# Prompt delta rule in chunks of 128 tokens instead of 64, in a hybrid decoder step

## The chip, the core and the metric

The kernel runs on one core of a Trainium2 chip. The core has a matrix engine (TensorE, PE in the profile; PEld is its loading of weights), a vector engine (VectorE, DVE), a scalar engine (ScalarE, ACT), GpSimd (POOL) and SyncE (SP), whose queue issues most DMAs. The engines run side by side and wait for each other by semaphores. The metric is the device time of one execution in microseconds; the median of several runs counts.

## The reference: what is computed

One layer of a decoder step, for a prompt of 256 tokens and for 8 decode sequences of one token each. One input projection feeds two token mixers: a sparse attention (compressed, selected and sliding-window branches) and a gated delta rule of 8 heads with a convolution ahead. Each mixer's output is gated and projected, the two are merged by gates, and an output projection is added to the input. The change touches the delta rule of the prompt:

```
def step(S, xc):                       # one chunk of C tokens, C = 64
    qc, kc, vc, gc, bc = xc
    dec = jnp.cumsum(gc, axis=-1)
    L = jnp.exp(jnp.where(tril, dec[..., :, None] - dec[..., None, :], -jnp.inf))
    ...
    A = jnp.where(stril, jnp.einsum('bhik,bhjk->bhij', kb, kc) * L, 0.0)
    Tm = lax.linalg.triangular_solve(eye + A, ...)      # the inverse
    u = Tm @ vb
    w = Tm @ (kb * jnp.exp(dec)[..., None])
    vn = u - w @ S
    att = jnp.where(tril, jnp.einsum('bhik,bhjk->bhij', qc, kc) * L, 0.0)
    o = (qc * jnp.exp(dec)[..., None]) @ S + att @ vn
    S = S * jnp.exp(dl)[..., None] + jnp.einsum('bhck,bhcv->bhkv', kc * jnp.exp(dl - dec)[..., None], vn)
    return S, o
```

The result of the recurrence does not depend on the length of a chunk. Heads have 128 key and 128 value channels; all of it is fp32.

## The kernel before

The body of the program is one long stream of weights. Each half of a weight unit (128 columns, 8 blocks of 128 rows, 512 KB) is loaded by SP into one of three buffers `raw`, split by ScalarE and VectorE into a high and a low fp32r part (`hi`, L326, and `lo`, L327), and used in 24 matmuls of 128x128x264, `acc` in the profile. `main order` at the end of the program lists the halves; load runs four halves ahead, the split two.

Everything else is written as Python generators (`g_gdn` for the prompt's delta rule, `g_gdn_dec` for that of the decode sequences, others for attention). Between two parts of a half, `tick` lets each of them emit the next piece, up to its next `yield n`, which asks for n ticks of rest. A scheduler then orders the instructions of TensorE, VectorE and ScalarE; SP and GpSimd keep the order of the program. When the stream comes to the first unit of the output gate of the delta rule (`ev_z` with w = 1), all that is left of `g_gdn` and `g_gdn_dec` is emitted at once, since that unit needs `oB`, their result.

`g_gdn`, in its order, for two tiles `t` of 128 tokens with two chunks of 64 in each: decays by matmuls with masks (`tric`, `bones`); for each head `At` (A transposed) and `aT` (att transposed) from one PSUM tile `kk`; the inverses of the 32x32 diagonal blocks of A, on VectorE by rows, one block a partition, through DRAM and back into `U` (the transposed inverse) and `TI`; a merge of 32x32 blocks to 64x64 ones by two groups of products (`inv` in the profile, copies `P`); for each head u and w (PSUM tile `uw`: four matmuls); then the scan over four chunks, each in two groups of four heads: `vn` = u - w S, `dS` (the growth of the state), `og` (the output), with the state in `Sg`. In the profile the state stands under the name `prod`, and vn and `aT` share the tile `aT`.

In the scan a chunk's 64 tokens are 64 partitions. So vn uses weights of 128 rows and 64 columns, dS of 64 rows and 128 columns, the first product of og 128 rows and 64 columns, and its second 64 by 64:

```
mm(pv[rows, 128 * hh:128 * hh + 128], wT[:, h, tok], Sg[:, h, :])
...
mm(pS[:, 128 * hh:128 * hh + 128], ktk[rows, t, h, :], vn[rows, h, :])
...
if c:
    mm(po[rows, ...], qTg[:, h, tok], Sg[:, h, :], start=True, stop=False)
mm(po[rows, ...], aT[rows, t, h, :], vn[rows, h, :], start=c == 0, stop=True)
```

The scan's and the merge's PSUM tiles come from one pool of two (`PG`). `sw` and `vnb` in the rows are matmuls and transpositions of `g_gdn_dec`, whose states `sst` (1 MB each, four of them) SP loads.

Of the kernel before, what the change touches and what calls it, by code (L numbers as in the profile page):

```python
# [49 lines left out]
def shape_constants():  # L50
    c = Cols()
    p = np.arange(128)
    same = (p[:, None] // 64) == (p[None] // 64)
    c.add("ident", np.eye(128))
    c.add("ones", np.ones((128, 128)))
    c.add("tric", (p[:, None] <= p[None]) & same)
    c.add("bones", same)
    c.add("mlow", np.where((p[:, None] > p[None]) & same, 0.0, BIG))
    c.add("mup", np.where((p[:, None] <= p[None]) & same, 0.0, -BIG))
    k = np.arange(256)  # L60
    q = p + 128
    c.add("base", np.where(q[:, None] >= k[None], -(q[:, None] - k[None]), -BIG))
    kend = np.arange(15) * 16 + 31
    b15 = np.zeros((128, 2, 15))
    for t in range(2):
        d = (p + 128 * t)[:, None] - kend[None]
        b15[:, t] = np.where(d >= 0, -d, -BIG)
    c.add("base15", b15)
    slope = 2.0 ** -(np.arange(8) + 1.0)
    c.add("slp", np.broadcast_to(np.tile(slope, 2) / SCALE, (128, 16)))  # L70
    kendd = np.arange(NCMP) * 16 + 31
    sl64 = np.broadcast_to(slope.reshape(2, 1, 4), (2, NB, 4)).reshape(64)
    c.add("cmpb", -(PAST - kendd)[:, None] * sl64[None])
    row = np.arange(64)
    srow = slope[(row // 32) * 4 + row % 4]
    c.add("c64", srow[:, None] * np.arange(64)[None])
    c.add("wrow", srow[:, None] * (np.arange(8) * 64 - 512)[None])
    c.add("e64", (row[None] // 4) == np.arange(16)[:, None])
    c.add("sel", ((row[None, None] // 32) == np.arange(2)[None, :, None])
          & (((row[None, None] // 4) % 8) == np.arange(8)[:, None, None]))  # L80
    c.add("rmask", ((p[:, None] % 64) // 4) == np.arange(16)[None])
    c.add("e", (np.arange(120)[None] // 8) == np.arange(16)[:, None])
    cs = np.arange(NCMP) * 16
    ss = np.arange(33) * 64
    ov = np.minimum(cs[:, None] + 32, ss[None] + 64) - np.maximum(cs[:, None], ss[None])
    c.add("m", (np.clip(ov, 0, None) / 32.0)[:, 1:31])
    c.add("gm", np.eye(24))
    dm = np.zeros((128, 8, NB))
    for h in range(8):
        dm[32 + h, h] = 1  # L90
        dm[64 + h, h] = 1
    c.add("dm", dm)
    c.add("s13", np.broadcast_to(np.arange(13), (16, 13)))
    c.add("blk", np.broadcast_to(np.arange(1, 31), (16, 30)))
    c.add("tg", (np.arange(120) % 8)[:, None] + (np.arange(16)[None] // 8) * (160 * 16))
    return c
# [42 lines left out]
def program(tc, A):  # L139
# [36 lines left out]

    # constants
    cst = cp.tile([128, CST.n], F32, name="cst")
# [39 lines left out]

    # long-lived small tiles
    xh = st.tile([128, KC, TT], F32R, name="xh", tag="xh")  # L220
# [50 lines left out]

    # ---- x: rms norm, split
    def g_xnorm():
# [34 lines left out]

    # ---- streams
    def three(ps, wh, wl, h, l, start, stop, n):  # L310
# [165 lines left out]

    # ---- projections
    def ev_kvc(j):
# [150 lines left out]

    # ---- decode: compressed attention, selection, gathers  # L630
    def g_dec_cmp():
# [41 lines left out]
        del L["kcT"], L["vc"]  # L673
        # ranks
        sa = slot("selA", [16, 2, 30, 30])
# [296 lines left out]

    # ---- prompt attention
    def g_attn():
# [6 lines left out]
        kT, vt = L["kTa"], L["vt"]  # L981
        # compressed branch, all heads
        z = tp.tile([128, 2, 8, 15], F32, name="pz", tag="pz")
# [91 lines left out]

    # ---- gated delta net
    def ev_qkv(j):
# [75 lines left out]
    def g_gdn():  # L1153
# [8 lines left out]
        bed = tp.tile([128, 2, 8], F32, name="bed", tag="bed")  # L1162
        edl = tp.tile([128, 8, 4], F32, name="edl", tag="edl")
        pt = PG("dec")
        for t in range(2):
            mm(pt[:, 8 * t:8 * t + 8], C("tric"), gt[:, t, :])
            mm(pt[:, 16 + 8 * t:24 + 8 * t], C("bones"), gt[:, t, :])
        V.tensor_copy(dec, pt[:, 0:16].rearrange("p (t h) -> p t h", t=2))
# [4 lines left out]
        At = slot("At", [128, 2, 8, 128])  # L1173
        av_ = slot("aT", [128, 2, 1024])
        aT = av_[:, 0].rearrange("p (t h i) -> p t h i", t=2, h=8)
        vn = av_[:, 1].rearrange("p (h d) -> p h d", h=8)
        yield 7
        lm = {}
        for h in range(9):
            if h < 8:  # L1180
# [13 lines left out]
                S.activation(l2, l2, AF.Exp)  # L1194
                V.tensor_copy(edl[:, h, :], er.rearrange("p (c i) -> p c i", c=4)[:, :, 63])
                lm[h] = l1, l2, er
            yield
            if h:
                h1 = h - 1
                l1, l2, er = lm.pop(h1)  # L1200
                pk = PG("kk")
                for t in range(2):
                    sl = slice(128 * t, 128 * t + 128)
                    mm(pk[:, 128 * t:128 * t + 128], kTg[:, h1, sl], kTg[:, h1, sl])
                    mm(pk[:, 256 + 128 * t:384 + 128 * t], kTg[:, h1, sl], qTg[:, h1, sl])
                for t in range(2):
                    V.scalar_tensor_tensor(At[:, t, h1, :], pk[:, 128 * t:128 * t + 128], be[:, t, h1:h1 + 1], l1[:, t],
                                           ALU.mult, ALU.mult)
                for c in range(2):
                    pr = slice(64 * c, 64 * c + 64)  # L1210
                    V.tensor_mul(aT[pr, :, h1, :], pk[pr, 256:512].rearrange("p (t i) -> p t i", t=2)[:, :, pr],
                                 l2[pr, :, pr])
                V.tensor_tensor(qTg[:, h1, 0:TP], qTg[:, h1, 0:TP], er, ALU.mult)
            yield 4
        del L["qkv", 1], kTg
        # inverse of the 32x32 diagonal blocks, one block a partition
        ad = dp.tile([4, 16, 32, 32], F32, name="ad")
# [32 lines left out]
        for t in range(2):  # L1250
            for hg in range(2):
# [16 lines left out]
                for c in range(2):  # L1268
                    V.tensor_scalar(U[64 * c:64 * c + 32, t, 4 * hg:4 * hg + 4, 64 * c + 32:64 * c + 64],
                                    p2v[64 * c:64 * c + 32, :, c, :], -1.0, None, ALU.mult)  # L1270
        uu = vbt
        wT = slot("wT", [128, 8, 256])
# [14 lines left out]
        del L["vbt"]  # L1287
        # scan
        Sg = prod[:, 0:1024].rearrange("p (h d) -> p h d", h=8)
        oG = slot("oG", [128, 2, 8, 128])  # L1290
        for c in range(4):
            t, off = c // 2, 64 * (c % 2)
            rows = slice(off, off + 64)
            tok = slice(64 * c, 64 * c + 64)
            for hg in range(2):
                hs = slice(4 * hg, 4 * hg + 4)
                if c == 0:
                    V.tensor_copy(vn[rows, hs], uu[rows, t, hs])
                else:
                    pv = PG("vn")  # L1300
                    for hh in range(4):
                        h = 4 * hg + hh
                        mm(pv[rows, 128 * hh:128 * hh + 128], wT[:, h, tok], Sg[:, h, :])
                    V.tensor_sub(vn[rows, hs], uu[rows, t, hs], pv[rows, :].rearrange("p (h d) -> p h d", h=4))
            yield 6
            for hg in range(2):
                hs = slice(4 * hg, 4 * hg + 4)
                pS = PG("dS")
                for hh in range(4):
                    h = 4 * hg + hh  # L1310
                    mm(pS[:, 128 * hh:128 * hh + 128], ktk[rows, t, h, :], vn[rows, h, :])
                yield 6
                po = PG("og")
                for hh in range(4):
                    h = 4 * hg + hh
                    if c:
                        mm(po[rows, 128 * hh:128 * hh + 128], qTg[:, h, tok], Sg[:, h, :], start=True, stop=False)
                    mm(po[rows, 128 * hh:128 * hh + 128], aT[rows, t, h, :], vn[rows, h, :],
                       start=c == 0, stop=True)
                yield  # L1320
                for hh in range(4):
                    h = 4 * hg + hh
                    if c == 0:
                        V.tensor_copy(Sg[:, h, :], pS[:, 128 * hh:128 * hh + 128])
                    else:
                        V.scalar_tensor_tensor(Sg[:, h, :], Sg[:, h, :], edl[:, h, c:c + 1],
                                               pS[:, 128 * hh:128 * hh + 128], ALU.mult, ALU.add)
                for hh in range(4):
                    h = 4 * hg + hh
                    S.activation(oG[rows, t, h], po[rows, 128 * hh:128 * hh + 128], AF.Copy, scale=qss[rows, t, h:h + 1])  # L1330
                yield 4
# [122 lines left out]

    # ---- output side
    hl = {}
# [58 lines left out]

    # ---- main order
    halves = []
# [202 lines left out]
```

## Time and profile before

| | |
|---|---|
| median of 3 runs | 1166.74 us (1165.35 to 1169.48) |
| the profiled execution, its span | 1167.3 us |
| TensorE, matmul | 1135.1 us busy, 97% |
| TensorE, weight load | 1097.8 us, 94% |
| VectorE / ScalarE / GpSimd | 68% / 52% / 13% |
| chain that ended last | TensorE 82%, VectorE 5%, DMA 3% |
| HBM | 203 MB read, 18 MB written, 189 GB/s |

The shares are means over the whole span. The chain that ended last follows the work back from the last instruction; what stands in it, and not what is busy, sets the time. A busy TensorE is not TensorE at its peak: the ends of matmuls are modelled and neighbours overlap, so the start of one call to that of the next tells more than a duration. The line L199 is the helper `mm` and L196 the helper `tr` (transposition on TensorE), through which nearly all matmuls go; the groups have to be read by their tiles. A matmul in fp32 leaves two records, so "x8" is four of them.

### The profile page before, as it was taken

To read this page: it belongs to the slowest core of one execution; us is meant where nothing else is said; L and a number is where in the kernel's file an instruction comes from. 1 tells how busy PE (TensorE), PEld (TensorE's weight loads), DVE (VectorE), ACT (ScalarE), POOL (GpSimd) and SP (SyncE) were. 2 spreads that over 40 slices of the span, in tenths; PEclk is the share of its full clock that TensorE was granted. 3 is DMA by queue.
4 is the path that set the end of the run, shared out by engine and by line. 5 is a ranking of instruction groups with operands and counts; after the bars stand their busy time and mean duration, and the time that the engine had idled before them with its cause. 6 is when DMAs were issued, how large, how long until landed. Compare 5 with 4: busy or idle time off the path is not lost.

```text
span 1167.3 us, 24685 instructions
## 1 busy us (share of the span) xinstructions
PE 1135.1 (97%) x9136; PEld 1097.8 (94%) x9136; DVE 789.7 (68%) x1651; ACT 607.6 (52%) x1173; POOL 147.5 (13%) x218
## 2 busy tenths in 40 slices
PE   3999999999999999999899999998999999999998
PEld 3989999999999997998899999998998799999998
DVE  3487665443677876986888876899575665567543
ACT  4455655444635776875666554443345354344332
POOL 4420344100001221204112100100100000000000
PEclk9999999999999999999999999999999999999999
DMA  8874576334436865468887644554743345555663
GB/s 296 256 223 148 191 217 203 106 133 164 159 133 198 227 181 147 135 192 210 320 316 269 245 162 162 188 204 134 231 172 118 127 145 179 183 181 210 206 237 128
DMA packets 76844, 222.83 MB, mean 191 GB/s; under 512 B 10465, under 2 KB 27370, under 8 KB 75186
## 3 DMA queue, kind: packets, MB, share of 16 engines
q1 hardware_dynamic: 59922, 168.55, 42.7%
q0 software_dynamic: 14784, 45.68, 13.6%
q10 hardware_dynamic: 2016, 7.01, 1.5%
q8 instruction: 72, 1.18, 0.4%
q14 instruction: 50, 0.41, 0.1%
HBM read 203.21 MB, written 17.99 MB: 189 GB/s over the span
## 4 chain that ended last, share of the span: by engine, by line
PE 82%; DVE 5%; DMA 3%; issue 1%; POOL 1%; ACT 1%; SPq 0%; DVEq 0%; ACTq 0%; POOLq 0%
PE acc L199 66%; PE og L199 2%; DMA gv<-cslv,idx 2%; DVE lo L327 1%; DVE lanes L1234 1%; PE po L199 1%; PE gsc L199 1%; PE gtr L196 1%; PE sw L199 1%; DVE prod L1233 1%; PE ps L199 1%; PE pvo L199 1%; DMA raw<-win 1%; PE dS L199 1%; PE cf L199 1%
## 5 line engine op out<-in xcount | busy, mean ns | idle before, releaser
L326 ACT ACTIVATE hi<-raw 128x1024 fp32r<-128x1024 f32 (+1 forms) x250 | 264.1, 1056 | 324.2 <-PE acc L199 260.5
L199 PE MATMUL acc<-xh,hi 128*128 128x264 f32 (+1 forms) x1488 | 428.5, 288 | 1.4 <-DVE gate L1489 1.0
L199 PE MATMUL acc<-xl,hi 128*128 128x264 f32 (+1 forms) x1488 | 426.6, 287 | 0.0
L199 PE MATMUL acc<-xh,lo 128*128 128x264 f32 (+1 forms) x1488 | 425.9, 286 | 0.0
L327 DVE TENSOR_TENSOR lo<-raw,hi 128x1024 fp32r<-128x1024 f32 (+1 forms) x250 | 304.5, 1218 | 172.1 <-ACT hi L326 168.5
L199 PEld LDWEIGHTS acc<-xh,hi 128*128 128x128 f32 (+1 forms) x1488 | 280.3, 188 | 3.8 <-ACT hi L326 1.2
L199 PEld LDWEIGHTS acc<-xl,hi 128*128 128x128 f32 (+1 forms) x1488 | 280.4, 188 | 1.9 <-issue 0.7
L199 PEld LDWEIGHTS acc<-xh,lo 128*128 128x128 f32 (+1 forms) x1488 | 279.5, 188 | 2.0 <-issue 1.0
L199 PE MATMUL acc<-hi,w1h 128*128 128x254 f32 (+1 forms) x512 | 147.6, 289 | 16.5 <-ACT hi L403 16.5
L199 PE MATMUL acc<-lo,w1h 128*128 128x254 f32 (+1 forms) x512 | 146.4, 286 | 3.8 <-DVE lo L404 3.6
L199 PE MATMUL acc<-hi,w1l 128*128 128x254 f32 (+1 forms) x512 | 144.9, 283 | 0.0
L404 DVE TENSOR_TENSOR lo<-rawc,hi 128x512 fp32r<-128x512 f32 (+2 forms) x136 | 84.0, 656 | 51.1 <-ACT hi L403 45.3
L199 PEld LDWEIGHTS acc<-hi,w1h 128*128 128x128 f32 x512 | 97.8, 191 | 16.8 <-ACT hi L403 16.7
L403 ACT ACTIVATE hi<-rawc 128x512 fp32r<-128x512 f32 (+2 forms) x136 | 74.6, 599 | 58.6 <-PE acc L199 54.4
L199 PEld LDWEIGHTS acc<-lo,w1h 128*128 128x128 f32 x512 | 98.3, 192 | 5.1 <-DVE lo L404 4.9
L199 PEld LDWEIGHTS acc<-hi,w1l 128*128 128x128 f32 x512 | 98.3, 192 | 0.1
L380 POOL DMA_DIRECT2D rawc<-ccmp x125 | 67.4, 539 | 100.4 <-issue 70.0
L199 PE MATMUL acc<-oh,hi 128*128 128x264 f32 x256 | 72.9, 285 | 0.4 <-ACT gate L1482 0.4
L199 PE MATMUL acc<-ol,hi 128*128 128x264 f32 x256 | 72.7, 284 | 0.0
L199 PE MATMUL acc<-mh,hi 128*128 128x264 f32 x256 | 72.6, 284 | 0.0
L199 PE MATMUL acc<-oh,lo 128*128 128x264 f32 x256 | 72.6, 283 | 0.0
L199 PE MATMUL acc<-ml,hi 128*128 128x264 f32 x256 | 72.5, 283 | 0.0
(447 smaller groups left out, 1685.2 us busy)
## 6 DMA issues: line engine op xcount, KB each, us to landing
raw<-win SPq DMA_DIRECT2D x184, 512.0 KB, 3.8
raw<-wpab SPq DMA_DIRECT2D x32, 512.0 KB, 3.2
raw<-wo SPq DMA_DIRECT2D x32, 512.0 KB, 4.3
rawc<-ccmp SPq DMA_DIRECT2D x126, 128.0 KB, 3.1
rawc<-ccmp POOLq DMA_DIRECT2D x125, 128.0 KB, 3.1
raw<-w SPq DMA_DIRECT2D x8, 512.0 KB, 8.0
wk<-winK SPq DMA_DIRECT2D x8, 512.0 KB, 7.4
o_wk<-wk POOLq DMA_DIRECT2D x8, 512.0 KB, 7.8
```

Source lines behind the costliest of these rows:

```text
L196: T.transpose(out, in_, ident[0:n, 0:n])
L199: T.matmul(out, lhsT, rhs, start=start, stop=stop, **k)
L326: S.activation(self.hi, self.raw, AF.Copy)
L327: V.tensor_sub(self.lo, self.raw, self.hi)
L380: e.dma_start(rawc[kv, b][j // 8][:, j % 8].rearrange("p s c g -> p (s c g)"), src[kv, bass.ds(r, 1)].rearrange("o d f -> (o d) f"))
L403: S.activation(h, src, AF.Copy)
L404: V.tensor_sub(l, src, h)
L1233: V.tensor_tensor(pp, Lt[:, 0:i, 0:i], La[:, i, 0:i, None].to_broadcast([64, i, i]), ALU.mult)
L1234: V.tensor_reduce(Lt[:, i, 0:i], pp.rearrange("p j c -> p c j"), AX.X, ALU.add, negate=True)
```

## The change

The delta rule of the prompt works on chunks of 128 tokens, so a chunk is a whole tile.

- The masks are those of 128 tokens; `bones` is replaced by the existing `ones`. `aT` holds 128x128 for each tile and head, and its product with the decays is one VectorE instruction instead of two.
- The inverse gets one more merge, of 64x64 blocks to 128x128: for each tile and each half of the heads four matmuls and four transpositions of 64x64, two copies on ScalarE (`P1`, `T1`), four matmuls of 64x64, and a negating copy on VectorE into `U`.
- The scan has two chunks instead of four, with all 128 partitions. The first chunk needs no vn; the one step that depends on a state is that of the second. vn is written in place into u (`uu`, in the profile `vbt`), the copy of the first chunk's u is gone, and the state of the first chunk is copied for four heads at once.
- The yields are others: 112 ticks of rest in the scan become 40, and 16 come with the merge.

```diff
-    c.add("tric", (p[:, None] <= p[None]) & same)
-    c.add("bones", same)
-    c.add("mlow", np.where((p[:, None] > p[None]) & same, 0.0, BIG))
-    c.add("mup", np.where((p[:, None] <= p[None]) & same, 0.0, -BIG))
+    c.add("tric", p[:, None] <= p[None])
+    c.add("mlow", np.where(p[:, None] > p[None], 0.0, BIG))
+    c.add("mup", np.where(p[:, None] <= p[None], 0.0, -BIG))
...
-                for c in range(2):
-                    pr = slice(64 * c, 64 * c + 64)
-                    V.tensor_mul(aT[pr, :, h1, :], pk[pr, 256:512].rearrange("p (t i) -> p t i", t=2)[:, :, pr],
-                                 l2[pr, :, pr])
+                V.tensor_mul(aT[:, :, h1, :], pk[:, 256:512].rearrange("p (t i) -> p t i", t=2), l2)
...
+        for t in range(2):
+            for hg in range(2):
+                p1 = PG("inv")
+                for hh in range(4):
+                    h = 4 * hg + hh
+                    mm(p1[0:64, 256 + 64 * hh:320 + 64 * hh], At[64:128, t, h, 0:64], U[64:128, t, h, 64:128])
+                for hh in range(4):
+                    tr(p1[0:64, 64 * hh:64 * hh + 64], U[0:64, t, 4 * hg + hh, 0:64])
+                yield 2
+                P1 = tp.tile([128, 256], F32, name="P1", tag="a", bufs=NA)
+                T1 = tp.tile([128, 256], F32, name="T1", tag="a", bufs=NA)
+                S.activation(P1[0:64], p1[0:64, 256:512], AF.Copy)
+                S.activation(T1[0:64], p1[0:64, 0:256], AF.Copy)
+                yield 2
+                p2 = PG("inv")
+                for hh in range(4):
+                    o = slice(64 * hh, 64 * hh + 64)
+                    mm(p2[0:64, o], T1[0:64, o], P1[0:64, o])
+                V.tensor_scalar(U[0:64, t, 4 * hg:4 * hg + 4, 64:128], p2[0:64, 0:256].rearrange("p (h j) -> p h j", h=4),
+                                -1.0, None, ALU.mult)
...
-        for c in range(4):
-            t, off = c // 2, 64 * (c % 2)
-            rows = slice(off, off + 64)
-            tok = slice(64 * c, 64 * c + 64)
...
+        for t in range(2):
+            tok = slice(128 * t, 128 * t + 128)
+            if t:
...
-                        mm(pv[rows, 128 * hh:128 * hh + 128], wT[:, h, tok], Sg[:, h, :])
-                    V.tensor_sub(vn[rows, hs], uu[rows, t, hs], pv[rows, :].rearrange("p (h d) -> p h d", h=4))
-            yield 6
+                        mm(pv[:, 128 * hh:128 * hh + 128], wT[:, h, tok], Sg[:, h, :])
+                    V.tensor_sub(uu[:, t, hs], uu[:, t, hs], pv.rearrange("p (h d) -> p h d", h=4))
+                yield 4
+            vn = uu[:, t]
...
-                    mm(pS[:, 128 * hh:128 * hh + 128], ktk[rows, t, h, :], vn[rows, h, :])
-                yield 6
+                    mm(pS[:, 128 * hh:128 * hh + 128], ktk[:, t, h, :], vn[:, h, :])
+                yield 4
...
-                    if c:
-                        mm(po[rows, 128 * hh:128 * hh + 128], qTg[:, h, tok], Sg[:, h, :], start=True, stop=False)
-                    mm(po[rows, 128 * hh:128 * hh + 128], aT[rows, t, h, :], vn[rows, h, :],
-                       start=c == 0, stop=True)
+                    if t:
+                        mm(po[:, 128 * hh:128 * hh + 128], qTg[:, h, tok], Sg[:, h, :], start=True, stop=False)
+                    mm(po[:, 128 * hh:128 * hh + 128], aT[:, t, h, :], vn[:, h, :], start=t == 0, stop=True)
```

How the instructions stand on the engines after scheduling. On TensorE, where the old merge ends and the products with `U` begin, the program before has:

```order
L199 MATMUL inv<-P_12769,prod 32x32 x8
L199 MATMUL uw<-vbt,U 128x128
L199 MATMUL uw<-U,kbe 128x128
L199 MATMUL uw<-vbt,U 128x128
L199 MATMUL uw<-U,kbe 128x128
L199 MATMUL acc<-ol,hi 128x264
```

After the change the new level begins there. This is its first round, and the start of the stream behind it:

```order
L197 MATMUL inv<-P_12761,prod 32x32 x8
L197 MATMUL inv<-U,At 64x64 x4
L194 MATMUL inv<-cst,U 64x64 x4
L197 MATMUL acc<-ol,hi 128x264
L197 MATMUL acc<-oh,lo 128x264
```

and the place where its last products (P and T are the copies P1 and T1) lead on to uw:

```order
L197 MATMUL inv<-P_13023,T_13024 64x64 x4
L197 MATMUL uw<-vbt,U 128x128
L197 MATMUL uw<-U,kbe 128x128
L197 MATMUL uw<-vbt,U 128x128
L197 MATMUL uw<-U,kbe 128x128
L197 MATMUL acc<-xh,hi 128x264
```

The first uw has moved behind four rounds of the new level. Between a round's first group and its last stand 26 acc calls, and the last products of the first three rounds stand together with the first of the next. The last uw comes 44 acc calls later than before. On TensorE in the scan, the first chunk that has a state stands before as:

```order
L199 MATMUL vn<-prod,wT 64x128 x4
L199 MATMUL sw<-wq,sst 128x64 x5
L199 MATMUL vn<-prod,wT 64x128 x4
L199 MATMUL sw<-wq,sst 128x64 x6
L199 MATMUL dS<-aT,ktk 128x128 x4
L199 MATMUL sw<-wq,sst 128x64 x3
L199 MATMUL og<-prod,qkvr 64x128
L199 MATMUL og<-aT 64x128
```

and after the change, where it is the only chunk that has one:

```order
L197 MATMUL sw<-wq,sst 128x64 x11
L197 MATMUL vn<-prod,wT 128x128 x4
L197 MATMUL dS<-vbt,ktk 128x128 x4
L197 MATMUL sw<-wq,sst 128x64 x5
L194 MATMUL vnb<-cst,dvn 128x128 x4
L197 MATMUL og<-prod,qkvr 128x128
L197 MATMUL og<-vbt,aT 128x128
```

The sizes are those of the output: 64 partitions have become 128. Such a place stands three times in the program before and once after. On SP's queue, where the second to fourth decode states are loaded ahead of the next weight halves, with the semaphores that each load waits for, before:

```order
L321 DMA raw<-win 128x1024 [waits DMAHW7_49,DVE_49]
L1414 DMA sst<-stS 128x2048 [waits DMASW3_49,DMASW4_49,DMASW2_49,DMASW6_49,DMASW1_49,DMASW7_49,DMASW0_49,PE_49]
L1414 DMA sst<-stS 128x2048 [waits DMASW5_49,PE_49]
L1414 DMA sst<-stS 128x2048 [waits DMASW4_49,DMASW3_49,DMASW5_49,DMASW2_49,DMASW7_49,DMASW0_49,PE_49]
L321 DMA raw<-win 128x1024 [waits DMAHW0_49,DVE_49]
```

and after:

```order
L319 DMA raw<-win 128x1024 [waits DMAHW7_49,DVE_49]
L1423 DMA sst<-stS 128x2048 [waits DMASW5_49,DMASW4_49,DMASW6_49,DMASW3_49,PE_49]
L1423 DMA sst<-stS 128x2048 [waits DMASW3_49,DMASW4_49,DMASW2_49,DMASW6_49,DMASW1_49,DMASW7_49,DMASW0_49,PE_49]
L1423 DMA sst<-stS 128x2048 [waits DMASW3_49,DMASW4_49,DMASW2_49,DMASW5_49,DMASW0_49,DMASW7_49,DVE_49,PE_49]
L319 DMA raw<-win 128x1024 [waits DMAHW0_49,Activation_49]
```

The order on SP is unchanged. The third of these loads goes, before and after, into the buffer of `U`, and so waits for the last uw on TensorE; the buffers of the first two have changed (after: that of an old weight operand, and that of `At`). The first half behind them is the same half, and its first acc call the same call, in both programs.

## Rows read from the trace of the kernel before

**Rows 1.** The page's engine line: busy us, share of the span, instructions.

```profile
PE 1135.1 (97%) x9136; PEld 1097.8 (94%) x9136; DVE 789.7 (68%) x1651; ACT 607.6 (52%) x1173; POOL 147.5 (13%) x218
```

**Rows 2.** Windows: merge and uw, scan, rest; us busy by engine, granted clock, DMA.

```profile
832.00:872.00 40.00, 39.57 (x382) 38.85 (x383) 26.05 (x69) 19.12 (x39) 0.00 (x0) 1.00 0.45 162
872.00:941.00 69.00, 69.00 (x499) 56.30 (x499) 40.74 (x123) 30.80 (x98) 0.17 (x1) 1.00 0.34 129
941.00:1167.00 226.00, 223.13 (x1848) 222.92 (x1846) 128.45 (x173) 95.75 (x128) 0.40 (x1) 1.00 0.54 187
```

**Rows 3.** Timeline of TensorE at one uw: start us, us, what, count of records.

```profile
858.35 0.28 PE L199 MATMUL acc<-xh,lo 128*128 128x264 f32 x1
858.47 0.38 PE L199 MATMUL uw<-vbt,U 128*128 128x128 f32 x2
...
859.49 0.28 PE L199 MATMUL acc<-xl,hi 128*128 128x264 f32 x1
```

**Rows 4.** Timeline of TensorE at one dS group (64*128: rows and columns of weights).

```profile
872.06 0.28 PE L199 MATMUL acc<-xh,lo 128*128 128x264 f32 x1
872.27 1.16 PE L199 MATMUL dS<-aT,ktk 64*128 64x128 f32 x8
...
873.58 0.28 PE L199 MATMUL acc<-xl,hi 128*128 128x264 f32 x1
```

**Rows 5.** Timeline of TensorE at one vn group.

```profile
922.05 0.28 PE L199 MATMUL acc<-xh,lo 128*128 128x264 f32 x1
922.26 1.09 PE L199 MATMUL vn<-prod,wT 128*64 128x128 f32 x8
...
923.50 0.28 PE L199 MATMUL acc<-xl,hi 128*128 128x264 f32 x1
```

**Rows 6.** Timeline of TensorE at one og group with a state.

```profile
929.54 0.28 PE L199 MATMUL acc<-xl,hi 128*128 128x264 f32 x1
929.75 0.43 PE L199 MATMUL og<-prod,qkvr 128*64 128x128 f32 x2
930.12 0.43 PE L199 MATMUL og<-aT 64*64 64x128 f32 x2
...
932.87 0.28 PE L199 MATMUL acc<-xh,hi 128*128 128x264 f32 x1
```

**Rows 7.** Timeline of TensorE at eight transpositions of attention, 64 rows.

```profile
507.96 0.68 PE L196 MATMUL ptr<-cst,sb 64*120 64x64 f32 x8
...
508.80 0.28 PE L199 MATMUL acc<-xl,hi 128*128 128x264 f32 x1
```

**Rows 8.** Timeline of TensorE at four such transpositions.

```profile
628.49 0.46 PE L196 MATMUL ptr<-cst,wb 64*128 64x64 f32 x4
...
629.11 0.28 PE L199 MATMUL acc<-xl,hi 128*128 128x264 f32 x1
```

**Rows 9.** Timeline of TensorE in the old merge: eight 32x32 matmuls.

```profile
836.32 0.44 PE L199 MATMUL inv<-P,prod 32*32 32x32 f32 x16
836.69 1.10 PE L199 MATMUL inv<-U,At 128*128 128x64 f32 x8
```

**Rows 10.** Timeline of ScalarE in the old merge: a split, then the copy P.

```profile
833.66 1.06 ACT L326 ACTIVATE hi<-raw 128x1024 fp32r<-128x1024 f32 x1 [0.31 <-DMA raw<-win]
834.63 0.36 ACT L1259 ACTIVATE P<-inv 128x256 f32<-128x256 f32 x1
```

**Rows 11.** Waits of SP's queue, 640 to 1000 us: us, times, longest.

```profile
SPq L1414 <- PE sw L199: 12.6, 1, 12.6
```

**Rows 12.** Loads of decode states (tile sst), whole trace.

```profile
DMA to landing us min/median/max: 7.4/8.0/8.5
```

**Rows 13.** DMA issues, 840 to 960 us: weight halves, KB, median us to landing.

```profile
raw<-win SPq DMA_DIRECT2D x19, 512.0 KB, 3.3
```

**Rows 14.** The page's groups of the split: busy us, mean ns of one.

```profile
L326 ACT ACTIVATE hi<-raw 128x1024 fp32r<-128x1024 f32 (+1 forms) x250 | 264.1, 1056 | 324.2 <-PE acc L199 260.5
L327 DVE TENSOR_TENSOR lo<-raw,hi 128x1024 fp32r<-128x1024 f32 (+1 forms) x250 | 304.5, 1218 | 172.1 <-ACT hi L326 168.5
```

More of the change, by code (lines that the diff above doesn't have):

```diff
@@ L52, in shape_constants @@
     p = np.arange(128)
-    same = (p[:, None] // 64) == (p[None] // 64)
     c.add("ident", np.eye(128))
     c.add("ones", np.ones((128, 128)))
-    c.add("tric", (p[:, None] <= p[None]) & same)
-    c.add("bones", same)
-    c.add("mlow", np.where((p[:, None] > p[None]) & same, 0.0, BIG))
-    c.add("mup", np.where((p[:, None] <= p[None]) & same, 0.0, -BIG))
+    c.add("tric", p[:, None] <= p[None])
+    c.add("mlow", np.where(p[:, None] > p[None], 0.0, BIG))
+    c.add("mup", np.where(p[:, None] <= p[None], 0.0, -BIG))
     k = np.arange(256)
@@ L1162, in g_gdn @@
         bed = tp.tile([128, 2, 8], F32, name="bed", tag="bed")
-        edl = tp.tile([128, 8, 4], F32, name="edl", tag="edl")
+        edl = tp.tile([128, 8, 2], F32, name="edl", tag="edl")
         pt = PG("dec")
@@ L1166, in g_gdn @@
             mm(pt[:, 8 * t:8 * t + 8], C("tric"), gt[:, t, :])
-            mm(pt[:, 16 + 8 * t:24 + 8 * t], C("bones"), gt[:, t, :])
+            mm(pt[:, 16 + 8 * t:24 + 8 * t], ones, gt[:, t, :])
         V.tensor_copy(dec, pt[:, 0:16].rearrange("p (t h) -> p t h", t=2))
@@ L1173, in g_gdn @@
         At = slot("At", [128, 2, 8, 128])
-        av_ = slot("aT", [128, 2, 1024])
-        aT = av_[:, 0].rearrange("p (t h i) -> p t h i", t=2, h=8)
-        vn = av_[:, 1].rearrange("p (h d) -> p h d", h=8)
+        aT = slot("aT", [128, 2, 8, 128])
         yield 7
@@ L1194, in g_gdn @@
                 S.activation(l2, l2, AF.Exp)
-                V.tensor_copy(edl[:, h, :], er.rearrange("p (c i) -> p c i", c=4)[:, :, 63])
+                V.tensor_copy(edl[:, h, :], er.rearrange("p (c i) -> p c i", c=2)[:, :, 127])
                 lm[h] = l1, l2, er
@@ L1290, in g_gdn @@
         oG = slot("oG", [128, 2, 8, 128])
-        for c in range(4):
-            t, off = c // 2, 64 * (c % 2)
-            rows = slice(off, off + 64)
-            tok = slice(64 * c, 64 * c + 64)
[L1295 to L1299, printed above, removed]
+        for t in range(2):
+            tok = slice(128 * t, 128 * t + 128)
+            if t:
+                for hg in range(2):
+                    hs = slice(4 * hg, 4 * hg + 4)
                     pv = PG("vn")
@@ L1315, in g_gdn @@
                     h = 4 * hg + hh
-                    if c:
-                        mm(po[rows, 128 * hh:128 * hh + 128], qTg[:, h, tok], Sg[:, h, :], start=True, stop=False)
-                    mm(po[rows, 128 * hh:128 * hh + 128], aT[rows, t, h, :], vn[rows, h, :],
-                       start=c == 0, stop=True)
+                    if t:
+                        mm(po[:, 128 * hh:128 * hh + 128], qTg[:, h, tok], Sg[:, h, :], start=True, stop=False)
+                    mm(po[:, 128 * hh:128 * hh + 128], aT[:, t, h, :], vn[:, h, :], start=t == 0, stop=True)
                 yield
[L1321 to L1326, printed above, removed]
+                if t == 0:
+                    V.tensor_copy(Sg[:, hs, :], pS.rearrange("p (h d) -> p h d", h=4))
+                else:
+                    for hh in range(4):
+                        h = 4 * hg + hh
+                        V.scalar_tensor_tensor(Sg[:, h, :], Sg[:, h, :], edl[:, h, t:t + 1],
                                                pS[:, 128 * hh:128 * hh + 128], ALU.mult, ALU.add)
@@ L1329, in g_gdn @@
                     h = 4 * hg + hh
-                    S.activation(oG[rows, t, h], po[rows, 128 * hh:128 * hh + 128], AF.Copy, scale=qss[rows, t, h:h + 1])
+                    S.activation(oG[:, t, h], po[:, 128 * hh:128 * hh + 128], AF.Copy, scale=qss[:, t, h:h + 1])
                 yield 4
```

## The prediction, made before the changed kernel had run

> **What bounds the kernel now.** I read the engine line of the page first: TensorE is busy 1135 of 1167 us, the other engines far less [rows 1]. Then the stretch that the change touches, by windows: the merge of the inverse and the products behind it (832 to 872 us), the scan (872 to 941) and the rest. TensorE is busy 39.57 of 40, 69.00 of 69 and 223.13 of 226 us, at full granted clock, while in the scan VectorE works 40.74 and ScalarE 30.80 us of 69, and the DMA engines a third of the time [rows 2]. So TensorE's own time is the price here: a microsecond of matmul less is a microsecond less, as long as nothing else comes to be waited for. A busy TensorE says nothing on how dense its calls are, so I took the rest from the timeline, from start to start.
>
> The weight stream, in fp32r, starts a call each 0.12 us (858.35 to 858.47) [rows 3]. The fp32 calls of the delta rule stand between those. What a group costs is the start of the second acc call behind it, minus the start of the last acc ahead, minus two steps of 0.12: what the change from the one kind of call to the other costs on either side is then in it. Four full calls (128 rows, 128 columns of weights, 128 moving columns) cost 859.49 - 858.35 - 0.24 = **0.90** us [rows 3]. Four half-height calls cost more: dS, with 64 rows, 873.58 - 872.06 - 0.24 = **1.28** [rows 4]; vn, with 64 columns, 923.50 - 922.05 - 0.24 = **1.21** [rows 5]. Worst are the eight calls of og behind the first chunk, where a call of 128 rows and one of 64 alternate: 932.87 - 929.54 - 0.24 = **3.09**, at 0.37 from each call to the next (929.75 to 930.12) [rows 6].
>
> **The change, part by part.**
>
> *The scan.* Four chunks of two head groups before: vn 6 groups (three chunks have a state) x 1.21 = 7.3; dS 8 x 1.28 = 10.2; og of the first chunk 2 groups, which I price as vn (64 columns, as many calls), 2.4; og of the other three 6 x 3.09 = 18.5. Together 38.4. Some dS and og stand side by side and pay the way in and out once; I take 1 off: 37.4. Afterwards there are two chunks: vn 2 groups of four, dS 4, og 2, and 2 of eight, which is 12 groups of four, all with full weights and 128 moving columns, the form of rows 3: 12 x 0.90 = 10.8. **The scan gives 26.6 us.** The alternation in og stays, but both its calls now have the form of uw.
>
> At this place a rule speaks against the change. The Trainium skill (TensorE: Matmul & The Clock Gate, LDWEIGHTS) says that a weight load takes time by its columns, whatever its rows. By it the 64-column loads of vn and og would be cheaper than the full ones, where the trace has 1.21 against 0.90; I go by the trace, and carry the rule as a rival.
>
> *The new level.* For each tile of 128 tokens and half of the heads: four matmuls (64 rows, 64 columns, 64 moving) and four transpositions into one PSUM bank, two copies by ScalarE, four matmuls, one negating copy by VectorE. A matmul leaves two records on TensorE (four vn are x8), a transposition one. So a round is 8 + 4 + 8 = 20 records, four rounds 80. No row of before has this form. The nearest are transpositions of 64 rows and 64 moving columns: eight take 508.80 - 507.96 - 0.12 = 0.72 [rows 7], four 629.11 - 628.49 - 0.12 = 0.50 [rows 8]; so 0.055 a record, and 0.28 for a run, to which I add the 0.09 of a late entry (872.06 to 872.27 is 0.21, not 0.12 [rows 4]): 0.37. By the new order the rounds make five runs, since each last product stands with the first products of the next round. 80 x 0.055 + 5 x 0.37 = **6.3 us**. From below: 32x32 calls, 16 records in 836.69 - 836.32 = 0.37 us [rows 9], give 80 x 0.023 = 1.8. From above: the price of vn, 0.151 a record, gives 12.1. I take 6.3, as rows and moving columns are equal there.
>
> *Waits that the level may add.* The order has 26 acc calls, 3.1 us, between a round's first products and its last. In that time ScalarE must make two copies. In the merge of before one such copy took 0.36 and began straight behind a 1.06 us weight split [rows 10]; two copies behind one split are 1.8 us. I allow 0.5 us for all waits, chosen, with 0 and 6 as ends (four rounds without cover, 1.5 each).
>
> *What costs nothing.* One attention product of 128 rows for two of 64, a two-column edl, one state copy for four, no vn copy, a smaller constant: on VectorE, GpSimd and at the start, and VectorE has 28 us to spare in the scan [rows 2]. If that cover were gone, the level's four negations and the joint copies would show; they replace more than they add.
>
> *Sum.* The profiled execution took 1167.3 us, 0.6 over the median of 1166.74. 1167.3 - 26.6 + 6.3 + 0.5 = 1147.5; against the median 1146.9. I say **1147**.
>
> **The rivals.**
>
> *The level is dearer.* At the price of vn 1153; with ScalarE's copies late in every round 1159. For it: copies queue behind splits of 1.06 us. Against: 3.1 us of cover against 1.8.
>
> *The level is cheaper.* At the price of the 32x32 calls 1142 to 1143. Against: those alternate between two sets of partitions (0 to 31, 64 to 95), the new ones stay on one set for four calls.
>
> *Half-width calls are half price.* If time went by columns of weights, with the full group at 0.90, vn and og would cost 0.45 and dS 0.90 before: 6 x 0.45 + 14 x 0.45 + 8 x 0.90 = 16.2 for the scan, which then gives only 5.4 and loses it to the level: 1168, no change. That is the rule named above. It would need the 1.21 of vn to be the price of its neighbours; but uw has the same neighbours and costs 0.90.
>
> *Weights come late, and it is slower.* On SP's queue three loads of decode state stand ahead of the next weight halves. Before, one of them waited 12.6 us for a buffer [rows 11], U's, which is free when the last uw has run. Now 44 more acc calls and the new level stand ahead of that uw, while the first acc that needs a withheld half is the same: 33 acc calls behind it instead of 77. Those, 4.0 us, and nine groups of four at 0.90 are 12.1 us of other work, decode calls not counted. Needed are 8.0 for a state load to land [rows 12], 3.3 for a weight half [rows 13] and the splits, 1.06 and 1.22 [rows 14]: 13.6. So it is near, and the uncounted decode calls should cover it. It decides the sign when the gap comes to 12.1 + 19.8 = 32 us; three state loads and three halves one after the other, 3 x 8.0 + 3 x 3.3 + 2.3 = 36 us, would give 1171. Against: only the third load waits for U, so the first two have long landed.
>
> **How the numbers follow.** Forecast (1143 to 1152) 0.63, dearer level (1152 to 1160) 0.22, cheaper (below 1143) 0.08, half-price calls 0.03, late weights 0.04. Range 1142 to 1156: it leaves out the last two, the upper part of the dearer level and the lower of the cheaper one, 0.18 in all. A measurement of this kernel can tell about 0.3%, 3.5 us, from no change. Faster are the first three, 0.93; same the half-price case, 0.03; slower late weights, 0.04.
>
> **What the new profile would show.** Groups of dS and vn at about 0.90 between acc calls and og's eight at about 1.8 make the first term right; 1.2 or 3 again make it wrong. The 64x64 records should start about 0.06 us apart within a run; 0.15 means the upper price. TensorE idle ahead of an inv call, released by ScalarE, is the missing cover; idle ahead of acc, released by a split of weights behind the last uw, is the late queue. TensorE's busy share should stay where it is, over a span some 20 us shorter. I am wrong if the scan's span shrinks by 26 us and the end does not move: then something else than TensorE ends it.

## The result, and the profile after

The changed kernel takes 1147.60 us in the median of four runs (1146.63 to 1149.08), the kernel before 1166.49 (1165.35 to 1169.48): a ratio of 0.9835, 95% interval 0.982 to 0.9851. It is faster by 18.9 us; the forecast was 1147. Two more sets of five runs of the changed kernel gave 1149.21 and 1147.42.

The page's engine line after the change, which answers to [rows 1] (busy us, share of the span, instructions):

```profile
PE 1116.5 (97%) x9088; PEld 1090.7 (95%) x9088; DVE 777.0 (68%) x1619; ACT 603.5 (53%) x1165; POOL 146.6 (13%) x218
```

TensorE's share is the same over a span of 1146.2 us, as forecast. The windows that answer to [rows 2] (merge, new level and uw; scan; rest):

```profile
831.00:882.00 51.00, 50.96 (x505) 48.70 (x505) 29.09 (x77) 22.37 (x48) 0.00 (x0) 1.00 0.37 126
882.00:912.00 30.00, 30.00 (x265) 29.91 (x263) 19.12 (x55) 20.93 (x77) 0.58 (x1) 1.00 0.60 216
912.00:1146.20 234.20, 231.01 (x1916) 230.80 (x1915) 137.49 (x208) 98.53 (x131) 0.00 (x0) 1.00 0.57 191
```

The scan has shrunk from 69 us to 30, acc calls among it included; the stretch ahead has grown by 11 us and the rest by 8, with more acc calls in both; TensorE is full in the first two, at full clock. In the list of TensorE's waits between 827 and 969 us there is nothing.

Now the groups that the prediction priced. A group of og in the first chunk, TensorE's timeline:

```profile
885.20 0.28 PE L197 MATMUL acc<-xh,lo 128*128 128x264 f32 x1
885.32 1.05 PE L197 MATMUL og<-vbt,aT 128*128 128x128 f32 x8
886.13 0.37 PE L197 MATMUL acc<-xh,hi 128*128 128x264 f32 x1
886.34 0.28 PE L197 MATMUL acc<-xl,hi 128*128 128x264 f32 x1
```

By the prediction's own measure this is 886.34 - 885.20 - 0.24 = 0.90 us, the price of uw in [rows 3]. The same group as 64x64 calls, in the kernel before, which the prediction had priced as vn without a row of its own:

```profile
874.31 0.28 PE L199 MATMUL acc<-xl,hi 128*128 128x264 f32 x1
874.52 1.08 PE L199 MATMUL og<-aT 64*64 64x128 f32 x8
...
875.76 0.28 PE L199 MATMUL acc<-xh,hi 128*128 128x264 f32 x1
```

It cost 875.76 - 874.31 - 0.24 = 1.21. And dS with the og behind it, in the chunk that has a state:

```profile
904.64 0.28 PE L197 MATMUL acc<-xh,hi 128*128 128x264 f32 x1
904.76 1.05 PE L197 MATMUL dS<-vbt,ktk 128*128 128x128 f32 x8
905.65 0.39 PE L197 MATMUL og<-prod,qkvr 128*128 128x128 f32 x2
905.87 0.39 PE L197 MATMUL og<-vbt,aT 128*128 128x128 f32 x2
...
907.44 0.27 PE L194 MATMUL vnb<-cst,dvn 128*128 128x128 f32 x1
```

dS takes 0.89 from its start to that of og (1.28 in [rows 4]), og's eight calls 1.79 (3.09 in [rows 6]), each 0.22 behind the one ahead. The two products of og still take turns and write the same sums; what has gone is the change of shape between them.

One round of the new level (last products of one round, `inv<-P,T`, then first products, `inv<-U,At`, and transpositions, `inv<-cst,U`, of the next):

```profile
852.33 0.28 PE L197 MATMUL acc<-xh,lo 128*128 128x264 f32 x1
852.55 0.50 PE L197 MATMUL inv<-P,T 64*64 64x64 f32 x5
...
852.94 0.22 PE L197 MATMUL inv<-U,At 64*64 64x64 f32 x1
852.95 0.22 PE L197 MATMUL inv<-P,T 64*64 64x64 f32 x1
...
853.44 0.41 PE L194 MATMUL inv<-cst,U 64*64 64x64 f32 x4
853.78 0.39 PE L197 MATMUL acc<-xh,hi 128*128 128x264 f32 x1
854.01 0.28 PE L197 MATMUL acc<-xl,hi 128*128 128x264 f32 x1
```

20 records in 853.78 - 852.55 = 1.23 us, 0.06 each, and 854.01 - 852.33 - 0.24 = 1.44 for the run with its way in and out: 0.055 a record and 0.37 a run had given 1.47. The two matmuls in the middle, on rows 64 to 127 and on rows 0 to 63, start 0.01 us apart: there the end of one group runs beside the start of the next. ScalarE in the same round, a split and then the two copies:

```profile
852.17 1.06 ACT L324 ACTIVATE hi<-raw 128x1024 fp32r<-128x1024 f32 x1 [2.21 <-PE acc L197]
853.95 0.38 ACT L1275 ACTIVATE P<-inv 64x256 f32<-64x256 f32 x1 [0.71 <-PE inv L194]
854.23 0.37 ACT L1276 ACTIVATE T<-inv 64x256 f32<-64x256 f32 x1
```

They start as soon as TensorE is done and end at 854.60; the products that read them start at 857.12. The cover has 2.5 us to spare.

### The profile page after: what moved, and what is told of

Read it like the earlier page. It is cut to its first block, busy times and chain, and to the rows that moved or that the text cites. A ratio compares the mean times of both kernels' runs of the same rounds, so it can differ in the third digit from the quotient of the medians.

```text
span 1146.2 us, 24552 instructions
## 1 busy us (share of the span) xinstructions
PE 1116.5 (97%) x9088; PEld 1090.7 (95%) x9088; DVE 777.0 (68%) x1619; ACT 603.5 (53%) x1165; POOL 146.6 (13%) x218
## 4 chain that ended last, share of the span: by engine, by line
PE 85%; DVE 4%; DMA 3%; issue 1%; ACT 1%; POOL 0%; ACTq 0%; POOLq 0%; DVEq 0%
PE acc L197 70%; DMA gv<-cslv,idx 2%; DVE lo L325 1%; PE po L197 1%; PE gsc L197 1%; PE gtr L194 1%; DVE lanes L1227 1%; PE ps L197 1%; PE sw L197 1%; DMA raw<-win 1%; PE inv L197 1%; PE cf L197 1%; DVE prod L1226 1%; PE pvo L197 1%; PE uw L197 1%
```

## The experiments

A run's time spreads by 2 to 3 us either way, as much as some of the effects. The traces are sharper. I counted acc calls, 24 to a weight half (those of the compression's own weights, `w1h` and `w1l`, left out), and cut each profiled execution at the start of the first acc call of half 158 (counted from 0; it lies ahead of everything that the change moves on TensorE) and of half 190 (behind it). Both cuts are the same calls in every kernel. In us, with the medians of the runs:

| kernel | to half 158 | 158 to 190 | to the end | median of runs |
|---|---|---|---|---|
| before | 828.3 | 161.7 | 177.3 | 1166.5 |
| before, again | 829.4 | 161.0 | 177.3 | 1167.4 |
| changed | 827.7 | 141.2 | 177.3 | 1147.6 |
| changed, again | 830.8 | 141.6 | 177.3 | 1149.2 |
| changed, third | 827.3 | 142.6 | 177.6 | 1147.4 |
| changed, table kept | 827.6 | 141.0 | 177.4 | 1148.5 |
| before + level | 826.4 | 167.3 | 177.3 | 1173.8 |
| changed - level | 832.4 | 135.4 | 177.3 | 1144.6 |
| before, og by shape | 827.4 | 155.6 | 177.3 | 1161.3 |
| before, vn x3 | 829.0 | 171.1 | 177.3 | 1177.8 |
| before, dS x3 | 828.2 | 174.4 | 177.3 | 1181.6 (one run) |
| changed, no first w | 830.6 | 140.3 | 177.3 | 1148.5 |
| the same, level in turns | 832.3 | 142.9 | 177.6 | 1154.1 |
| changed, state loaded x3 | 834.5 | 142.7 | 178.7 | 1154.0 |

The middle column is what the experiments are read by.

**The level, added to the kernel before and taken from the changed one.**

> The changed kernel itself, as the base for the runs beside it. All theories: 1147.6 us, 0.982 to 0.985 of before.

> The kernel before with the new merge level added and nothing else; its masks make the blocks that the level multiplies zero, so it writes zeros where zeros stand. My theory: the level costs what its 80 records and its five runs cost on TensorE, 6.05 us by the start-to-start times in the changed kernel (forecast 6.3), wherever it stands: 1166.5 + 6.1 = 1172.6, 1.0052 of before. Dearer level (0.151 a record, waits for the ScalarE copies): 1178 or more. Cheaper level (0.023 a record): 1168.3.

> The changed kernel without the new merge level: the part of the inverse between the two 64-token blocks of a tile is left out. My theory: the scan alone gives its 26.6 us less what comes with it, and the level's 6.05 us are gone: 1147.6 - 6.1 = 1141.5. Dearer level: 1136 or less. Rival, late weights: the products with U now come 44 acc calls earlier, so SP's queue is free earlier; if the queue cost time in the changed kernel, the gain is larger than 6.1, by the idle time of TensorE ahead of acc, which the trace shows as zero.

```diff
-        for t in range(2):
-            for hg in range(2):
-                p1 = PG("inv")
-                for hh in range(4):
-                    h = 4 * hg + hh
-                    mm(p1[0:64, 256 + 64 * hh:320 + 64 * hh], At[64:128, t, h, 0:64], U[64:128, t, h, 64:128])
...
```

(the changed kernel without the level; the same lines, up to the copy into `U`, are added to the kernel before ahead of `uu`.)

Measured: 1149.21, 1173.84 (1.0055, interval 1.0037 to 1.0072) and 1144.55 (0.9804, 0.9786 to 0.9821). In the middle column the level costs 167.3 - 161.7 = 5.6 or 167.3 - 161.0 = 6.3 on the kernel before, and 141.2 - 135.4 = 5.8 in the changed one (6.2 against the second profile). It costs the same in both surroundings. (The median without the level is 3 us over its forecast of 1141.5; its profile was late already at half 158, 832.4.) Its round on the kernel before has the same rows:

```profile
855.45 0.28 PE L199 MATMUL acc<-xl,hi 128*128 128x264 f32 x1
855.66 0.50 PE L199 MATMUL inv<-P,T 64*64 64x64 f32 x5
...
856.55 0.41 PE L196 MATMUL inv<-cst,U 64*64 64x64 f32 x4
856.89 0.39 PE L199 MATMUL acc<-xh,lo 128*128 128x264 f32 x1
857.12 0.28 PE L199 MATMUL acc<-xh,hi 128*128 128x264 f32 x1
```

857.12 - 855.45 - 0.24 = 1.43. The dearer level (12) and the cheaper one (1.8) are both out. And the scan by itself gives 161.7 - 135.4 = 26.3, or 25.6 from the second profile.

**og's calls in the order of their shape.**

> The kernel before with og's eight calls in the order of their shape (four of 128 rows, then four of 64) and each starting its own sum, so that the state's part of the output is overwritten and left out; as many calls of the same shapes. My theory: 0.37 a call in the alternating groups is the price of changing the shape; one change for seven saves 6 x 0.145 = 0.87 a group and 5.2 us in all: 1161.3. Rival: each of the two shapes has its own price of 0.3 to 0.37, whatever stands beside it: 1166.5.

```diff
                 for hh in range(4):
                     h = 4 * hg + hh
                     if c:
-                        mm(po[rows, ...], qTg[:, h, tok], Sg[:, h, :], start=True, stop=False)
-                    mm(po[rows, ...], aT[rows, t, h, :], vn[rows, h, :], start=c == 0, stop=True)
+                        mm(po[rows, ...], qTg[:, h, tok], Sg[:, h, :], start=True, stop=True)
+                for hh in range(4):
+                    h = 4 * hg + hh
+                    mm(po[rows, ...], aT[rows, t, h, :], vn[rows, h, :], start=True, stop=True)
```

Measured: 1161.31 us, 0.9946 (0.9929 to 0.9964). The middle column falls by 5.4 to 6.1. TensorE's timeline at one such group:

```profile
924.94 1.09 PE L199 MATMUL og<-prod,qkvr 128*64 128x128 f32 x8
925.96 1.08 PE L199 MATMUL og<-aT 64*64 64x128 f32 x8
926.98 0.39 PE L199 MATMUL acc<-xh,hi 128*128 128x264 f32 x1
```

2.04 us from 924.94 to 926.98 for the eight calls, where [rows 6] has 0.37 from call to call. Over all og records, from the start of each to the start of the next, 19.35 us became 14.22: 5.1 us for 36 changes of shape less, 0.14 each. The Trainium skill (TensorEngine Tiling (Array Packing), Tiling Modes, Key Properties) says that changing the tiling mode drains TensorE; the trace agrees that a change costs, 0.14 us, and does not show the draining itself. That each sum is started anew here can hardly be the reason: in the changed kernel the two products take turns within a sum at 0.22 a call.

**Half-width and half-height calls, three times as many.**

> The kernel before with each vn group issued three times, 48 more calls with 128 rows and 64 columns of weights, behind calls of their own shape. My theory: the excess of 1.21 over 0.90 is paid on the way in and out, and a call inside costs what a full one does, 0.225: 10.8 more, 1177.3. Half price by columns, the rival of the prediction: 0.112 a call, 5.4 more, 1171.9. Each call is dear (1.21 / 4 = 0.30): 14.5 more, 1181.

> The kernel before with each dS group issued three times, 64 more calls with 64 rows and 128 columns. My theory (way in and out, 0.225 a call inside): 14.4 more, 1180.9. Each call is dear (1.28 / 4 = 0.32): 20.5 more, 1187. Price by columns alone: 14.4 as well.

```diff
-                    for hh in range(4):
+                    for hh in (0, 1, 2, 3) * 3:
                         h = 4 * hg + hh
                         mm(pv[rows, 128 * hh:128 * hh + 128], wT[:, h, tok], Sg[:, h, :])
```

(and the same at dS in the other.) Measured: 1177.81 (1.0092, 1.0061 to 1.0122) and, in one run, 1181.55. The rows of the tripled groups:

```profile
928.67 5.45 PE L199 MATMUL vn<-prod,wT 128*64 128x128 f32 x48
934.06 0.65 PE L196 MATMUL vnb<-cst,dvn 128*128 128x128 f32 x4
```

```profile
935.27 2.94 PE L199 MATMUL dS<-aT,ktk 64*128 64x128 f32 x24
938.14 0.43 PE L199 MATMUL og<-prod,qkvr 128*64 128x128 f32 x2
```

24 vn calls in 5.39 us are 0.22 each, 12 dS calls in 2.87 are 0.24, with the way out in both. In the middle column 48 more vn calls cost 9.4 to 10.1, 64 more dS calls 12.7 to 13.4: 0.20 to 0.21 a call, near the 0.22 of a full one. So a call with half the columns, or half the rows, is no cheaper and inside a run no dearer; what was dear was the way into and out of its shape. The rule on columns that the prediction carried as a rival (the Trainium skill, TensorE: Matmul & The Clock Gate, LDWEIGHTS) does not set the price of these fp32 calls: by it 5.4 would have come, and 9.4 to 10.1 did. For the loads by themselves it holds in the rows: columns count and rows do not (ns, shortest, median and longest; a full load of uw takes 192):

```profile
L199 PEld LDWEIGHTS vn<-prod,wT x48: 133/137/137, 882.8 to 924.8; 128*64 128x64 f32 x48
L199 PEld LDWEIGHTS dS<-aT,ktk x64: 182/188/188, 872.3 to 937.2; 64*128 64x128 f32 x64
```

vn's shorter loads buy nothing in the price of its calls.

**w of the first tile.**

> The changed kernel without w for the first tile, which nothing reads now that the first chunk is a whole tile without a state: eight full matmuls and eight VectorE instructions less, half of each ScalarE copy. My theory: 8 x 0.90 / 4 = 1.8 us less, 1145.8. Rival: in that stretch the copies of u and w and two PSUM tiles set the pace and not TensorE; then no change, 1147.6.

```diff
             for t in range(2):
                 mm(pu[:, 128 * t:128 * t + 128], U[:, t, h, :], vbt[:, t, h, :])
-                mm(pu[:, 256 + 128 * t:384 + 128 * t], kb[:, t], U[:, t, h, :])
+                if t:
+                    mm(pu[:, 384:512], kb[:, 1], U[:, t, h, :])
...
-            S.activation(wT[:, h, :], pu[:, 256:512], AF.Copy)
+            S.activation(wT[:, h, 128:256], pu[:, 384:512], AF.Copy)
```

Measured: 1148.49 (0.9839, 0.9816 to 0.9861) beside 1149.21, which can't be told apart. The trace shows 140.3 for the middle, 0.9 to 1.3 less than the first two profiles of the changed kernel (141.2 and 141.6). The rest of the 1.8 went into this:

```profile
874.55 0.71 PE L197 MATMUL uw<-vbt,U 128*128 128x128 f32 x4 [0.16 <-ACT wT L1299]
...
876.32 0.71 PE L197 MATMUL uw<-vbt,U 128*128 128x128 f32 x4 [0.15 <-ACT wT L1299]
```

With a quarter less to do for a head (three matmuls for four), TensorE now waits for ScalarE's copies out of the two PSUM tiles; the uw records as a whole take 1.3 us less, these waits included. So both theories hold in part: what is gained is a little over half of the forecast, and too small for the time of a run to show.

**The level's calls in turns.**

> The changed kernel without w for the first tile (as in the run on that alone, whose time from the 158th to the 190th half was 140.3 us) and with the level's first products (rows 64 to 127 of the array) and its transpositions (rows 0 to 63) in turn, one of each for a head. If calls on different rows overlap, as the 32x32 calls of the old merge seem to (0.023 us a record against 0.06 to 0.08 in the level), the twelve records of a round take some 0.3 us less, 1.2 us for the four rounds: 139.1 in that stretch, 1146 to 1147 us in all. If they don't overlap: 140.3 and 1147 to 1148. If the turn from matmul to transposition costs what a change of shape costs, 0.145: seven changes for one, 0.9 a round, 3.5 us more: 143.8.

```diff
                 for hh in range(4):
                     h = 4 * hg + hh
                     mm(p1[0:64, 256 + 64 * hh:320 + 64 * hh], At[64:128, t, h, 0:64], U[64:128, t, h, 64:128])
-                for hh in range(4):
                     tr(p1[0:64, 64 * hh:64 * hh + 64], U[0:64, t, 4 * hg + hh, 0:64])
```

Measured: 1154.10 (0.9896, 0.9872 to 0.992); the middle is 142.9 against 140.3, 2.6 more. The third case it was:

```profile
852.65 0.32 PE L197 MATMUL inv<-U,At 64*64 64x64 f32 x2
852.91 0.24 PE L194 MATMUL inv<-cst,U 64*64 64x64 f32 x1
853.08 0.32 PE L197 MATMUL inv<-U,At 64*64 64x64 f32 x2
853.34 0.24 PE L194 MATMUL inv<-cst,U 64*64 64x64 f32 x1
```

Each pair takes 0.43 us. A round's run costs 2.26 where it cost 1.43: 0.83 for six more turns, 0.14 each, as much as a change of shape, though all these calls are 64x64. Four rounds of that are 3.3; the middle shows less also because a wait of 0.5 for a gate of VectorE, in the profile without w, is not in this one. The change of rows by itself is not what costs: in the round of the changed kernel above, matmuls on rows 64 to 127 and on rows 0 to 63 start 0.01 us apart (852.94 and 852.95). But those write two PSUM tiles, and the calls here write one; whether it is the turn from matmul to transposition or the common tile, no run tells.

**The decode state loaded three times on SP's queue.**

> The changed kernel with the fourth decode state loaded three times, one load behind the other on SP's queue, ahead of the withheld weight halves; nothing is left out. In the changed kernel TensorE does not wait for these halves, and the high part of the first of them is ready 1.7 us before it is needed. Late weights are near: two loads of 4.6 to 7.7 us move the halves by 9 to 15 us, and TensorE waits for what is over the slack, some 2 to 10 us: 1150 to 1158. Late weights are far: no change, 1147.6.

```diff
-            SP.dma_start(ss, A["stS"][b0 // 2])
+            for _ in range(3 if b0 == 6 else 1):
+                SP.dma_start(ss, A["stS"][b0 // 2])
```

Measured: 1154.04 (0.9882, 0.9851 to 0.9913). Most of that lies ahead of the edit (834.5 to half 158, the latest of all profiles), and why is not shown. The waits on SP's queue and, in the second fence, on TensorE (us, times, longest):

```profile
SPq L1424 <- PE uw L197: 14.4, 1, 14.4
SPq L1424 <- DMA sst<-stS: 9.4, 2, 5.0
```

```profile
PE acc L197 <- ACT hi L324: 0.7, 1, 0.7
PE acc L197 <- DVE lo L325: 0.4, 1, 0.4
```

The weight halves came over 9 us later and TensorE waited 1.1 us for their splits. The middle is 1.1 to 1.5 over the first two profiles of the changed kernel (but as long as the third, 142.6), and what lies behind it 1.3 over the first: 2 to 3 us at most. It is less than the delay, also because the order on TensorE is another in this kernel: more calls of the decode part stand ahead of the late half. The edit delays the decode state as well as the halves, so the 1.1 us are not the price of late weights alone.

**Does the change cost something ahead of its place?** In the first sets the medians showed 18.9 and 17.8 us less, the middle column 20.0 to 20.5.

> The kernel before itself, profiled once more beside the next two. From the start to the first acc call of the 158th weight half, which lies ahead of everything that the change moves on TensorE, the first profile took 828.3 us, the two of the changed kernel 827.7 and 830.8. If this part differs by chance from one execution to the next, this profile lies anywhere between 826 and 833. If the change itself costs 1 to 2 us there, this profile lies at or below 828.3. Between the 158th and the 190th half it should give 161 to 162 us again, since that part repeated within 0.5 us in the changed kernel.

> The changed kernel with the table of constants at its old size (the mask bones is back in it, and nothing reads it), so that everything behind it on chip lies where it lay before. If the smaller table costs time ahead of the delta rule: 1 to 2 us faster than the changed kernel, which gave 1147.6 and 1149.2. By chance: no difference, 1147.5 to 1149.5.

> The changed kernel, for the third time, as the base of the run ahead. 1147.5 to 1149.5 by all theories; from the 158th to the 190th half 141 to 142 us; ahead of it 826 to 833 by chance, 829 or more if the change costs time there.

```diff
     c.add("tric", p[:, None] <= p[None])
+    c.add("bones", (p[:, None] // 64) == (p[None] // 64))
```

Measured, in this order: 1167.38 (1.0008, 0.9989 to 1.0028), 1148.49 (0.9849, 0.9829 to 0.987) and 1147.42 (0.9829, 0.9809 to 0.9849). The third changed profile reached half 158 at 827.3, the kernel before at 829.4. So that part differs by chance from one execution to the next, and the size of the table does nothing that can be measured (827.6 and 141.0 with the old size). The middle of the third profile, 142.6, has two waits in it that the first has not:

```profile
PE inv L197 <- DMA U<-td: 0.6, 1, 0.6
PE acc L197 <- DVE gate L1498: 0.6, 1, 0.6
```

With this profile the gain in the middle lies between 18.4 and 20.5 us.

## Why the prediction was right

*The scan, 26.6 forecast: 25.6 to 26.3 measured*, by the kernel without the level. The experiments also say what it consists of, for the greater part. The scan went from 112 calls (24 vn, 32 dS, 56 og) to 48. The 64 calls that are gone were worth 12.8 to 14.1, at the 0.20 to 0.22 of the tripled groups. The changes of shape within og were worth 5.1. What is left, 6.4 to 8.4, no run measured by itself; it fits the way into and out of 22 groups of another shape than acc's: 1.21 for four vn calls, less 4 x 0.22, is 0.33, and 22 x 0.33 = 7.3, an estimate. A group of the full shape pays almost nothing of it (0.90 against 0.88). The prediction had all three in its prices, without telling them apart.

*The new level, 6.3 forecast: 5.6 to 6.3 measured*, alone and in place. The transpositions of attention were a good row to go by, with some luck in how the price divides: in the round above a record cost 0.06, not 0.055, and the way in and out 1.44 - 1.23 = 0.21, not 0.37, and the two errors offset each other. The five runs came as forecast.

*Waits of the level, 0.5 forecast: none.* The copies began behind TensorE's calls, not behind a split, and ended some 2.5 us early in each of the four rounds.

*The sum.* 161.7 - 26.6 + 6.3 + 0.5 = 141.9 for the middle column; measured 141.2, 141.6 and 142.6. One step was loose: the 1167.3 us taken as the execution's time are its span, and a run's time is 1.7 to 1.9 above its span (1147.96 against 1146.2 for the profiled run of the changed kernel). By that the profiled execution of before stood 2 to 3 us over the median, not 0.6. The number given followed the median as well (1146.9), so it did no harm.

*Late weights, 0.04: it did not happen, but it was nearer than the prediction's account.* The third load waited for the last uw as forecast:

```profile
SPq L1423 <- PE uw L197: 14.4, 1, 14.4
```

The 12.6 of [rows 11] are the same wait in the kernel before, as the prediction took them, though the row names an sw. The last uw there, and the state loads with their first and last start:

```profile
870.29 0.39 PE L199 MATMUL uw<-U,kbe 128*128 128x128 f32 x2
L1414 SPq DMA_DIRECT2D sst<-stS x4: 328/351/425, 775.9 to 870.7; - x4
```

The last load is issued at 870.71, 0.03 us behind the end of the last uw (870.68), while the sw calls behind that uw still run. In the changed kernel the first withheld half was split and used so (timelines of ScalarE, VectorE and TensorE in the changed kernel):

```profile
896.60 1.05 ACT L324 ACTIVATE hi<-raw 128x1024 fp32r<-128x1024 f32 x1
899.26 1.22 DVE L325 TENSOR_TENSOR lo<-raw,hi 128x1024 fp32r<-128x1024 f32 x1
899.33 0.37 PE L197 MATMUL acc<-xh,hi 128*128 128x264 f32 x1
...
900.54 0.39 PE L197 MATMUL acc<-xh,lo 128*128 128x264 f32 x1
```

The low part is ready at 900.48, the first call that reads it starts at 900.54. Between the two acc calls shown first and last stand another acc call and eight vnb transpositions. SP issued the half at 882.72, 0.4 us behind the third state load, and it landed 6.8 us later, at 889.5. ScalarE, in whose order the copies of og's output stand ahead of this split, was waiting for an og then, was busy without a gap from 890.94 to 896.60 with outputs and decode states, and took the half late. So the prediction's account was off on three counts: it added up the landings of the state load and of the half (8.0 + 3.3), which run side by side; it left out what stands ahead of the split on ScalarE and VectorE; and the decode calls that it had not counted made the room 17.1 us (from the end of the last uw, 882.26, to 899.33), not 12.1. These calls were to cover the gap, and with both loads landed 7.2 us behind the last uw there was less to cover than it thought.

*Half-price calls, 0.03*: excluded by the tripled vn.

## What to carry to other kernels

Price a small matmul group from start to start between its neighbours, not by its rows, columns or busy time: here a call cost 0.22 us whatever half of the array it left empty, and each change of shape 0.14 us on top, so a recurrence cut into half-height chunks paid twice for its calls and again for each change. An extra level of small products costs its records and its runs; here it paid, 6 us for 26, because it took the calls behind it from 112 to 48. Where a run's time spreads by more than the effect, cut two traces at the same calls and compare the piece.

## What was not expected

Turning from a 64x64 matmul to a 64x64 transposition on other rows, and back, cost 0.14 us a turn, the same as a change of shape, while two 64x64 matmuls on those two sets of rows started 0.01 us apart, and 32x32 matmuls that take turns between rows 0 to 31 and 64 to 95 run at 0.023 [rows 9]. And three executions of one program reached the same call of the stream at 827.3, 827.7 and 830.8 us, while the 177.3 us of its last part repeated to 0.3 us.
